# Linear attention: the low-rank gate input by 32-column products on the unnormalized state

## The chip, the cores and the metric

One NeuronCore of a Trainium2 chip runs the whole program. The metric is the device time of one execution in microseconds, the median of several runs. TensorE (PE) multiplies, VectorE (DVE) and ScalarE (ACT) do the elementwise work, GpSimd (POOL) some sums and roots, and SyncE (SP) issues most transfers.

## The reference

A trunk of two layers over 16 meta tokens and 512 tokens, width 1024. Each layer is feed-forward, mixer, feed-forward, each of them with RMSNorm before and after. The first layer's mixer is the gated linear attention that the change touches:

```python
hn = rmsnorm(h, g[2])
q, k, v, r, lr = jnp.split(hn @ w_in, ...)          # 512, 512, 1024, 1024 and 16 columns
gk = log_sigmoid(lr @ w_gate + b_gate) / 16         # 512 columns: 4 heads of 128
bcum = cumsum(gk)                                   # within chunks
q_dec, k_dec = q * exp(bcum), k * exp(-bcum)
o = causal(q_dec @ k_dec.T) @ v + q_dec @ states    # states carried from chunk to chunk
o = rmsnorm(o, g_head) * silu(r)                    # per head, 256 columns each
mix = o @ w_out
```

The 16 columns `lr` are the low-rank input of the forget gate. All four heads need the gate before anything else of theirs can begin.

## The kernel before

The state is kept transposed: tile `H` has 128 rows (a slice of the width), 8 such blocks (`KD`), and 528 tokens in columns. Tokens are worked in two groups, 272 and 256 (`L0`).

**Exactness.** The large products are made of three passes: weights and activations are each split into a rounded part and a rest (`split_part`, L233 on ScalarE, L234 on VectorE; for activations `Operand.build`), and high x high, low x high, high x low are added in PSUM. `mm3s` issues them. `mm` issues one product; a tile of plain float32 goes through it as well.

**The norm.** `Operand.build` multiplies the state by the gain of its row block only. The factor 1/rms of each token is made beside the products (`sumsq`, `factors`, `root`, `rstd`) and multiplied in when a result leaves PSUM (`x.rt`, in the traces `R_l0m`). `x.rjob` are the jobs that deliver it for each group.

**Weights.** `units` lists all weight tiles in order of use. A unit of the attention is 128 columns of `w_in`, 512 KB, fetched by two transfers on the SP queue into a ring of 8 raw tiles, split into two pair tiles, and released after use. `GLA_ORDER` gives the order: 24 is the low-rank unit (16 columns, padded to 128), 0 to 3 are the queries, 4 to 7 the keys, 8 to 15 the value tiles (two for each head), 16 to 23 the output gates `r`.

**Order of work.** TensorE's list is written out by hand. `Flow` is a virtual clock: every product adds its planned cost, and jobs (generators) resume when their `yield` is due, so their products land between those of the main line. For the other engines a scheduler sets the order. On the chip the lists are fixed, and each engine works through its own, waiting where it must.

**The attention.** `gla` begins with `x_first`: four units at once, the first group for all four, then the second group, since the state's second half arrives late. Then `x_units` takes unit after unit (both groups, 48 products each). Beside this run:

- `gates`: waits until the low-rank columns have been evacuated, multiplies them with `w_gate` (tiles `z`), and makes log-sigmoids for all heads (`ls`).
- `core(h)`, one job for each head, each waiting for the gates, its values and the head before it: cumulative sums, transposes of the values (`pv`), decays, transposes of the keys (`pk`), scores (`pa`, `pb`), chunk states (`ps`), outputs (`po`, `pn`), then the head's RMSNorm: squares (`acc_go`), their sums by twelve products with one column (`st_go`), a root in ten small steps and a diagonal (`dg_go`), and a product that spreads it over the rows (`r_go`). For the last head the root is made on VectorE, for the others on GpSimd.
- `gated(m)`: evacuates an output-gate unit (`rg`), applies tanh (L1040 to L1042), waits for the head's core, and makes the split operand `og` (L426, L427).

After the last `r` unit `out_proj` multiplies `og` with the output weights (tiles `y`). While the x units last, their products fill TensorE between the steps of the cores.

Of the kernel before, what the change touches and what calls it, by code (L numbers as in the profile page):

```python
# [13 lines left out]
ALU = mybir.AluOpType  # L14
AX = mybir.AxisListType

P = 128
D = 1024
KD = 8
# [9 lines left out]
L0 = [(0, 272), (272, 256)]  # L29
# [17 lines left out]
LONGER = 0.8  # L47
BEHIND = 2.2
NORM = 4.0
LAG = 5  # L50
PERIOD = 3.2
SLOWER = 4.0
# [5 lines left out]
V_GAIN = 0  # L58
# [2 lines left out]
V_GN = 108  # L61
V_SINK = 110
V_N = 126
GLA_ORDER = [24, 4, 0, 8, 9, 5, 1, 10, 11, 6, 2, 12, 13, 7, 3, 14, 15] + list(range(16, 24))


class Flow:
# [63 lines left out]
def trunk_kernel(ctx: ExitStack, tc, a, out):  # L131
    nc = tc.nc
    pe, act, dve, pool, sp = nc.tensor, nc.scalar, nc.vector, nc.gpsimd, nc.sync
    flow = Flow()
# [7 lines left out]
    H = cp.tile([P, KD, TOK], F32, name="H")  # L142
    Y = cp.tile([P, KD, TOK], F32, name="Y")
    vec = cp.tile([P, V_N], F32, name="vec")
# [12 lines left out]
    def duo(name):  # L157
        t = pair_tile(name, F32)
        return t[:, 0], t[:, 1]
# [355 lines left out]
    def x_units(x, nu, groups, evac):  # L515
        late = []

        def drain(i, g, p):
            for job in x.rjob:
                yield job  # L520
            evac(i, g, p)

        raw = x.column is not None

        for i in range(nu):
            w = next_w()
            pst = [ps(f"x{used[0]}_{gi}") for gi in range(len(groups))]
            for k in range(KD):
                for g, p in zip(groups, pst):
                    mm3(p[:, : g[1]], w, k, x.tiles[k], g, k == 0, k == KD - 1)  # L530
            done_w()
            for g, p in zip(groups, pst):
                if raw or all(job.done for job in x.rjob):
                    evac(i, g, p)
                else:
                    late.append(flow.spawn(drain(i, g, p)))
        return late
# [313 lines left out]
    def gla(x, finish):  # L851
        set_ahead(10)
        with tc.tile_pool(name="gp", bufs=1) as gp:
            wg, att = duo("wg")
            wg = wg[:, :512]
# [8 lines left out]
            def resets():  # L864
# [2 lines left out]
                    pool.memset(mt[:, META::st], 0.0)  # L867
                pool.memset(att, 0.0)
                yield 0
            lr = duo("lr")[0]  # L870
            qk, ls = {}, {}

            def evac(kind, h, g, p):
                o, n = g
                r = x.rt[:, o : o + n]
                if kind == "lr":
                    dve.tensor_tensor(lr[:, o : o + n], p[:, :n], r, op=ALU.mult)
                elif kind in "qk":
                    if h not in qk:
                        qk[h] = duo(f"qk{h}")  # L880
                    d = qk[h][kind == "k"][:, o : o + n]
                    if kind == "q":
                        dve.scalar_tensor_tensor(d, p[:, :n], 128 ** -0.5, r, op0=ALU.mult, op1=ALU.mult)
                    else:
                        dve.tensor_tensor(d, p[:, :n], r, op=ALU.mult)
                else:
                    dve.tensor_tensor(Y[:, h, o : o + n], p[:, :n], r, op=ALU.mult)

            def gates(drained):
                for j in drained:  # L890
                    yield j
                yield 0.8
                mns = duo("ls01") + duo("ls23")
                pairs = [pair_tile(f"az{i}", F32) for i in range(2)]
                for i, az in enumerate(pairs):
                    for h in (2 * i, 2 * i + 1):
                        b = vec[:, V_BG + h : V_BG + h + 1]
                        for o, n in L0:
                            p = ps(f"z{h}_{o}")
                            mm(p[:, :n], wg[:, h * P : (h + 1) * P], lr[:, o : o + n])  # L900
                            act.activation(az[:, h % 2, o : o + n], p[:, :n], AF.Abs, bias=b)
                            dve.tensor_scalar(mns[h][:, o : o + n], p[:, :n], b, 0.0, op0=ALU.add, op1=ALU.min)
                    last = act.activation(az, az, AF.Tanh, scale=0.5)
                    yield 1.0
                for i, az in enumerate(pairs):
                    log = act.activation(az, az, AF.Ln, scale=0.5, bias=bhalf)
                    after(last, log)
                    for h in (2 * i, 2 * i + 1):
                        dve.tensor_tensor(mns[h], mns[h], az[:, h % 2], op=ALU.add)
                        ls[h] = mns[h]  # L910
                yield 2.0
# [135 lines left out]
                dve.scalar_tensor_tensor(gs, gs, gn, Y[:, m, o : o + n], op0=ALU.mult, op1=ALU.mult)  # L1047
                split(og[m], gs, g)

            kinds = [("lr", 0), ("k", 0), ("q", 0), ("v", 0)]  # L1050
            drained = x_first(x, 4, lambda i, g, p: evac(*kinds[i], g, p), first_ahead=5)
            flow.spawn(resets())
            gate = flow.spawn(gates(drained))
            late = x_units(x, 1, L0, lambda i, g, p: evac("v", 1, g, p))
            for h in range(HEADS):
                cores.append(flow.spawn(core(h, [gate] + late + cores[h - 1 : h])))
                if h + 1 < HEADS:
                    kk = [("k", h + 1), ("q", h + 1), ("v", 2 * h + 2), ("v", 2 * h + 3)]
                    late = x_units(x, 4, L0, lambda i, g, p, kk=kk: evac(*kk[i], g, p))
# [73 lines left out]
    def swa(x, kv, finish):  # L1133
        kz, vt, dv, vmz = kv
        cap[0] = used[0] + 8
        with tc.tile_pool(name="ap", bufs=1) as ap:
# [109 lines left out]
            def core(i):  # L1246
                yield softs[i]
                yield NORM
                u, hf = visits[i]
# [71 lines left out]
    x = Operand("l0f0", lambda k: gain(0, 0, k), L0, parts=(2, 2))  # L1321
# [54 lines left out]
    x = nxt  # L1376
    nxt, fin = into("l0f1", 0, 3, False, lambda k: gain(0, 4, k), L0)
    gla(x, fin)
    x = nxt
# [4 lines left out]
    with tc.tile_pool(name="kp", bufs=1) as kp:  # L1384
        x = Operand("l1f0", lambda k: gain(1, 0, k), L1)
# [12 lines left out]
        x = nxt  # L1398
# [16 lines left out]
def _tiles(w, kt, mt):  # L1415
    return w.reshape(kt, P, mt, P).transpose(2, 1, 0, 3).reshape(mt, P, kt * P)


def _layout(x, meta_tokens, norm_gains, w_ffn_in, w_ffn_out, gla_w_in, gla_w_gate, gla_b_gate, gla_norm,
            gla_w_out, kv_norm, w_kv, swa_w_q, swa_sinks, swa_w_out):  # L1420
    c = {}
    c["h"] = np.concatenate([meta_tokens, x[0]], axis=0).T.reshape(KD, P, TOK).transpose(1, 0, 2)
    c["w_in"] = (
        w_ffn_in.reshape(2, 2, KD, P, 2, NFF, P).transpose(0, 1, 5, 4, 3, 2, 6).reshape(2, 2, NFF, 2, P, D)
    )
    wo = w_ffn_out.reshape(2, 2, NFF, P, KD, P).transpose(0, 1, 4, 3, 2, 5)
    c["w_out"] = wo[:, :, :, :, :LAST].reshape(2, 2, KD, P, LAST * P)
    c["w_last"] = (
        wo[:, :, :, :, LAST:].transpose(0, 1, 2, 4, 3, 5).reshape(2, 2, NLAST, KD, P, P)
        .transpose(0, 1, 2, 4, 3, 5).reshape(2, 2, NLAST, P, D)  # L1430
    )
    gin = np.zeros((D, 25 * P), np.float32)
    gin[:, : gla_w_in.shape[2]] = gla_w_in[0]
    c["gla_in"] = _tiles(gin, KD, 25)
    wg = np.zeros((P, 512), np.float32)
    wg[:16] = gla_w_gate[0]
    c["w_gate"] = wg
    c["gla_out"] = _tiles(gla_w_out[0], KD, KD)
    c["w_kv"] = _tiles(w_kv, KD, 4)
    c["w_q"] = (  # L1440
        swa_w_q[0].reshape(KD, P, 2, 2, 4, 64).transpose(2, 4, 1, 0, 3, 5).reshape(KD, P, D)
    )
    c["swa_out"] = (
        swa_w_out[0].reshape(2, 2, 4, 64, 4, 2, P).transpose(0, 4, 1, 3, 5, 2, 6).reshape(KD, P, D)
    )
    vec = np.zeros((P, V_N), np.float32)
    vec[:, V_GAIN : V_GAIN + 96] = norm_gains.reshape(96, P).T
    vec[:, V_KVN : V_KVN + 8] = kv_norm.reshape(8, P).T
    vec[:, V_BG : V_BG + 4] = gla_b_gate[0].reshape(4, P).T
    vec[:, V_GN : V_GN + 2] = gla_norm[0].reshape(2, P).T  # L1450
    vec[:, V_SINK : V_SINK + 16] = np.broadcast_to(
        swa_sinks[0].reshape(2, 2, 4).transpose(0, 2, 1).reshape(1, 16), (P, 16)
    )
    c["vec"] = vec
    i, j = np.arange(P)[:, None], np.arange(P)[None, :]
    c["ident"] = np.eye(P, dtype=np.float32)
    c["gmask"] = ((i <= j) & (i // 64 == j // 64)).astype(np.int32)
    c["mgt"] = (j > i).astype(np.int32)
    c["mle"] = (i <= j).astype(np.float32)
    c["rowmask"] = (i // META == np.arange(8)[None, :]).astype(np.float32)  # L1460
    ang = np.arange(TOK, dtype=np.float32)[:, None] * np.array(INV_FREQ, np.float32)[None, :]
    cos, sin = np.cos(ang).T.astype(np.float32), np.sin(ang).T.astype(np.float32)
    ct, st = np.ones((P, TOK), np.float32), np.zeros((P, TOK), np.float32)
    for r in (0, 64):
        ct[r : r + 8], ct[r + 8 : r + 16] = cos, cos
        st[r : r + 8], st[r + 8 : r + 16] = -sin, sin
    c["cos"], c["sin"] = ct, st
    c["sel"] = np.zeros((P, 32), np.float32)
    for e in range(2):
        c["sel"][64 * e : 64 * e + 16, 16 * e : 16 * e + 16] = np.eye(16)  # L1470
    c["cosp"], c["sinp"] = np.tile(np.concatenate([cos, cos]), (8, 1)), np.tile(np.concatenate([-sin, sin]), (8, 1))
    return {n: np.ascontiguousarray(v) for n, v in c.items()}
# [20 lines left out]
```

## Time and profile before

| | us |
|---|---|
| median of 3 runs | 1905.15 (1903.95 to 1905.66) |
| profiled execution | 1903.94 |
| its span in the trace | 1902.2 |
| TensorE busy | 1878.5 |
| VectorE busy | 1403.7 |
| ScalarE busy | 1016.8 |
| attention: first x product to first output product | 375.8 to 577.4 |

Busy times are unions over the span; a row of the timeline gives start, length, engine, line, operation, result and operands, and the number of records. A product of plain float32 leaves two records, one of the split kind leaves one. A pair such as 128*32 after MATMUL is rows and columns of the array in use. A few records can be missing.

### The profile page before, as it was taken

What the parts mean: (1) busy time and instruction counts of PE and PEld (TensorE: products, weight loads), DVE (VectorE), ACT (ScalarE), POOL (GpSimd) and SP (SyncE); (2) the same over time, 40 slices, a digit from 0 to 9 for tenths busy, and PEclk for the clock granted to TensorE, in tenths of its full rate; (3) what the DMA queues carried; (4) which work ended last, traced back from release to release, by engine and by line L of the source; (5) the groups of instructions that cost most, each with busy time, mean ns of one, the idle gap of its engine ahead of it and who ended that gap; (6) DMA issues with size and microseconds to landing.
All of it is one profiled execution on the core that took longest, in us unless ns stands there. A gap on an engine that the chain in (4) does not pass through costs nothing.

```text
span 1902.2 us, 37641 instructions
## 1 busy us (share of the span) xinstructions
PE 1878.5 (99%) x14642; PEld 1796.4 (94%) x14642; DVE 1403.7 (74%) x2825; ACT 1016.8 (53%) x2268; POOL 187.8 (10%) x374
## 2 busy tenths in 40 slices
PE   8999999999999999999999999999999999999997
PEld 8999999999999999999999898989987798989897
DVE  7885858766574798585887886868766779868584
ACT  5663635653245566363674553535756755636363
POOL 2000000321111300000033000000320140000002
PEclk9999999999999999999999999999999999999999
DMA  4333333422123123333351223233421212333331
GB/s 166 98 97 98 97 105 98 126 79 73 50 63 105 46 88 92 94 103 98 101 172 45 67 89 112 92 110 99 134 73 51 68 45 73 105 104 107 101 112 45
DMA packets 102931, 175.13 MB, mean 92 GB/s; under 512 B 11872, under 2 KB 24928, under 8 KB 102752
## 3 DMA queue, kind: packets, MB, share of 16 engines
q1 hardware_dynamic: 101920, 172.07, 28.8%
q8 instruction: 115, 1.88, 0.4%
q10 hardware_dynamic: 832, 0.65, 0.1%
q14 instruction: 64, 0.52, 0.1%
HBM read 170.05 MB, written 2.10 MB: 91 GB/s over the span
## 4 chain that ended last, share of the span: by engine, by line
PE 86%; DVE 10%; ACT 2%; issue 2%; DMA 0%; POOL 0%; DVEq 0%; ACTq 0%; POOLq 0%
PE y L169 29%; PE x L169 18%; PE a L169 18%; PE c L169 8%; PE d L169 4%; DVE raw L258 2%; PE o L169 1%; ACT w_s L252 1%; DVE w_s L253 1%; DVE w L253 1%; PE e L169 1%; DVE w L234 1%; PE po L169 1%; PE sa L169 1%; PE ps L169 0%
## 5 line engine op out<-in xcount | busy, mean ns | idle before, releaser
L253 DVE TENSOR_TENSOR w_s<-raw,w_s 128x512 fp32r<-128x512 f32 x288 | 193.9, 691 | 130.5 <-ACT w_s L252 128.1
L169 PE MATMUL y<-hidl0f,w 128*128 128x256 f32 (+1 forms) x2112 | 262.3, 285 | 1.1 <-DVE hidl0f L427 0.8
L169 PEld LDWEIGHTS y<-hidl0f,w 128*128 128x128 f32 x2112 | 259.2, 188 | 2.2 <-DVE hidl0f L427 1.5
L252 ACT ACTIVATE w_s<-raw 128x512 fp32r<-128x512 f32 x288 | 175.1, 628 | 151.5 <-DVE raw L258 138.5
L234 DVE TENSOR_TENSOR w<-raw,w 128x512 fp32r<-128x512 f32 x378 | 236.4, 656 | 21.8 <-ACT w L233 19.9
L169 PE MATMUL y<-hidl1f,w 128*128 128x512 f32 (+1 forms) x1344 | 250.9, 346 | 0.4 <-DVE hidl1f L844 0.2
L169 PEld LDWEIGHTS y<-hidl1f,w 128*128 128x128 f32 x1344 | 212.5, 188 | 35.0 <-DVE hidl1f L844 1.6
L233 ACT ACTIVATE w<-raw 128x512 fp32r<-128x512 f32 x378 | 207.5, 586 | 40.1 <-PE y L169 29.3
L422 POOL TENSOR_TENSOR acc_post<-acc_post,sq_post 128x256 f32<-128x256 f32 (+1 forms) x77 | 63.2, 821 | 1473.1 <-ACT sq_post L421 1472.4
L258 DVE TENSOR_TENSOR raw<-raw,raw 128x512 f32<-128x512 f32 x288 | 198.0, 688 | 5.5
L253 DVE TENSOR_TENSOR w<-raw,w 128x512 fp32r<-128x512 f32 x216 | 148.4, 688 | 29.9 <-ACT w L252 29.1
L169 PE MATMUL x<-x_l0m,w 128*128 128x272 f32 (+1 forms) x1200 | 158.2, 288 | 0.0
L252 ACT ACTIVATE w<-raw 128x512 fp32r<-128x512 f32 x216 | 134.0, 621 | 41.3 <-PE y L169 41.0
L169 PEld LDWEIGHTS x<-x_l0m,w 128*128 128x128 f32 x1200 | 149.3, 189 | 1.0
L621 DVE TENSOR_TENSOR Y<-y,Y 128x256 f32<-128x256 f32 (+2 forms) x176 | 82.4, 474 | 73.1 <-PE y L169 72.6
L169 PE MATMUL a<-zl0f_t,w_s 128*128 128x264 f32 x864 | 117.3, 285 | 0.0
L169 PE MATMUL a<-zl1f_t,w_s 128*128 128x256 f32 x864 | 114.7, 282 | 0.8 <-ACT c L819 0.6
L169 PEld LDWEIGHTS a<-zl0f_t,w_s 128*128 128x128 f32 x864 | 110.2, 188 | 0.2
L169 PEld LDWEIGHTS a<-zl1f_t,w_s 128*128 128x128 f32 x864 | 107.4, 188 | 2.7 <-ACT c L819 2.2
L169 PE MATMUL x<-x_l0f,w 128*128 128x256 f32 (+1 forms) x768 | 100.3, 291 | 6.4 <-ACT w L233 5.8
L169 PEld LDWEIGHTS x<-x_l0f,w 128*128 128x128 f32 x768 | 97.1, 193 | 7.5 <-ACT w L233 5.8
L169 PE MATMUL x<-x_l1f,w 128*128 128x256 f32 (+1 forms) x576 | 93.1, 321 | 0.0
(497 smaller groups left out, 3249.0 us busy)
## 6 DMA issues: line engine op xcount, KB each, us to landing
raw<-in_w_in SPq DMA_DIRECT2D x352, 256.0 KB, 2.9
raw<-in_w_out SPq DMA_DIRECT2D x96, 256.0 KB, 3.4
raw<-in_gla_in SPq DMA_DIRECT2D x50, 256.0 KB, 3.2
raw<-in_w_last SPq DMA_DIRECT2D x48, 256.0 KB, 3.1
raw<-in_w_out SPq DMA_DIRECT2D x64, 128.0 KB, 2.9
raw<-in_gla_out SPq DMA_DIRECT2D x16, 256.0 KB, 2.8
raw<-in_w_q SPq DMA_DIRECT2D x16, 256.0 KB, 4.1
raw<-in_swa_out SPq DMA_DIRECT2D x16, 256.0 KB, 3.2
```

The source lines that it names most:

```text
L169: inst = pe.matmul(o, lhs, rhs, start=start, stop=stop, skip_group_check=onto)
L233: act.activation(w[:, 0, :m], raw[:, :m], AF.Copy)
L234: dve.tensor_tensor(w[:, 1, :m], raw[:, :m], w[:, 0, :m].bitcast(F32), op=ALU.subtract)
L252: act.activation(w[:, 0, :512], src, AF.Copy)
L253: dve.tensor_tensor(w[:, 1, :512], src, w[:, 0, :512].bitcast(F32), op=ALU.subtract)
L258: dve.tensor_tensor(dst, dst, src, op=ALU.add)
L422: pool.tensor_tensor(sums[0][:, :n], sums[0][:, :n], t[:, :n], op=ALU.add)
L621: dve.tensor_tensor(y, p[:, :n], y, op=ALU.add)
```

## The change

The low-rank columns are no longer a unit. Their weights come as 1024 x 32 columns (16 of them zeros) in a transfer of their own into the free half of tile `lr`; VectorE multiplies the gains into them. Then 16 plain float32 products, 8 row blocks for each token group, read the state `H` itself. Row blocks 0 to 3 go to four column strips of the array and four row strips of a PSUM bank, blocks 4 to 7 are added to them. The four partial sums are not added there: `w_gate` is laid out four times, 32 rows each, so that the gate product adds them. The evacuation multiplies by 1/rms, after waiting for both groups' factors.

In `x_first` the freed place is taken by the first head's second value tile, which had a pass of `x_units` of its own, so 24 units remain instead of 25. The gates wait for the new job as well.

```diff
-GLA_ORDER = [24, 4, 0, 8, 9, 5, 1, 10, 11, 6, 2, 12, 13, 7, 3, 14, 15] + list(range(16, 24))
+GLA_ORDER = [4, 0, 8, 9, 5, 1, 10, 11, 6, 2, 12, 13, 7, 3, 14, 15] + list(range(16, 24))
...
-            lr = duo("lr")[0]
+            lr, low = duo("lr")
+            low = low[:, : KD * 32].rearrange("p (k c) -> p k c", c=32)
+            sp.dma_start(low, a["w_low"])
...
-                if kind == "lr":
-                    dve.tensor_tensor(lr[:, o : o + n], p[:, :n], r, op=ALU.mult)
-                elif kind in "qk":
+                if kind in "qk":
...
+            def low_rank():
+                gains = vec[:, V_GAIN + 16 : V_GAIN + 16 + KD]
+                dve.tensor_tensor(low, low, gains.unsqueeze(2).to_broadcast([P, KD, 32]), op=ALU.mult)
+                yield LOW
+                banks = [ps(f"lr_{o}") for o, _ in L0]
+                for (o, n), p in zip(L0, banks):
+                    for k in range(KD):
+                        c = slice(k % 4 * 32, k % 4 * 32 + 32)
+                        mm(p[c, :n], low[:, k], H[:, k, o : o + n], k < 4, k >= 4, cost=0.14)
+                for job in x.rjob:
+                    yield job
+                for (o, n), p in zip(L0, banks):
+                    dve.tensor_tensor(lr[:, o : o + n], p[:, :n], x.rt[:, o : o + n], op=ALU.mult)
...
-            kinds = [("lr", 0), ("k", 0), ("q", 0), ("v", 0)]
+            kinds = [("k", 0), ("q", 0), ("v", 0), ("v", 1)]
             drained = x_first(x, 4, lambda i, g, p: evac(*kinds[i], g, p), first_ahead=5)
             flow.spawn(resets())
-            gate = flow.spawn(gates(drained))
-            late = x_units(x, 1, L0, lambda i, g, p: evac("v", 1, g, p))
+            gate = flow.spawn(gates(drained + [flow.spawn(low_rank())]))
+            late = []
...
-    gin = np.zeros((D, 25 * P), np.float32)
-    gin[:, : gla_w_in.shape[2]] = gla_w_in[0]
-    c["gla_in"] = _tiles(gin, KD, 25)
-    wg = np.zeros((P, 512), np.float32)
-    wg[:16] = gla_w_gate[0]
-    c["w_gate"] = wg
+    c["gla_in"] = _tiles(gla_w_in[0][:, : 24 * P], KD, 24)
+    low = np.zeros((D, 32), np.float32)
+    low[:, :16] = gla_w_in[0][:, 24 * P :]
+    c["w_low"] = low.reshape(KD, P, 32).transpose(1, 0, 2)
+    wg = np.zeros((4, 32, 512), np.float32)
+    wg[:, :16] = gla_w_gate[0]
+    c["w_gate"] = wg.reshape(P, 512)
```

More of the change, by code (lines that the diff above doesn't have):

```diff
@@ L49 @@
 NORM = 4.0
+LOW = 1.0
 LAG = 5
```

## The prediction

> **What bounds the kernel now.** I read the page first: the shares of busy time, then the chain that ended last.
>
> ```profile
> PE 1878.5 (99%) x14642; PEld 1796.4 (94%) x14642; DVE 1403.7 (74%) x2825; ACT 1016.8 (53%) x2268; POOL 187.8 (10%) x374
> PE 86%; DVE 10%; ACT 2%; issue 2%; DMA 0%; POOL 0%; DVEq 0%; ACTq 0%; POOLq 0%
> ```
>
> TensorE works for 99% of the span and is 86% of the chain. The waits of TensorE inside the attention stage (376 to 592 us) have one entry:
>
> ```profile
> PE y L169 <- DVE og L427: 0.4, 1, 0.4
> ```
>
> So in this stage a product that goes is time won, as long as something else stands where it stood; a product that covered a chain on another engine is not.
>
> **The unit that goes.** The low-rank columns were one of 25 units of 128 columns; a unit is 48 products (3 passes, 8 row blocks, two token groups). The timeline of TensorE has an undisturbed stretch of such products:
>
> ```profile
> 403.33 6.83 PE L169 MATMUL x<-x_l0m,w 128*128 128x272 f32 x54
> 410.00 0.59 PE L169 MATMUL r_l0m<-dg_l0m,ones 128*128 128x256 f32 x2
> ```
>
> 54 products fill 403.33 to 410.00, 0.123 us each; 48 of them are **-5.9 us**. The first head's second value unit only changes its place (from alone to within x_first), with the same 48 products. Two fewer splits on VectorE and ScalarE and 0.5 MB less on the queue are off the path.
>
> **The 16 products that come.** They are plain float32, 128 rows by 32 columns, four of them in four column strips. The trace has this shape once, in the rotary turn, and the unpacked float32 shape in the gates:
>
> ```profile
> 1392.89 0.64 PE L169 MATMUL turn<-q,sel 128*32 128x256 f32 x8
> 1393.46 1.80 PE L169 MATMUL x<-x_l1m,w 128*128 128x256 f32 x13
> 1441.75 1.07 PE L169 MATMUL turn<-q,sel 128*32 128x512 f32 x8
> 417.70 1.94 PE L169 MATMUL z<-lr,wg 128*128 128x272 f32 x8
> 419.30 4.36 PE L169 MATMUL x<-x_l0m,w 128*128 128x256 f32 x33
> ```
>
> Eight records are four products (two records each). Packed, four take 0.57 us from their start to the next work (1393.46 - 1392.89); unpacked, four take 1.60 (419.30 - 417.70). So the strips do run side by side, and four groups of four cost 4 x 0.57 = **+2.3 us**. The lower end is 4 x 0.43 = 1.7 us, 0.43 being what 256 more columns cost the group (1.07 - 0.64); the upper end is 4 x 1.60 = 6.4 us. I take 2.3, the row of the same shape. The gate products keep number and size: the four partial sums are added by the repeated gate weights.
>
> **What they wait for.** The weights come by a transfer queued on SP behind that of the gate weights, into a slot freed some two microseconds later; VectorE then multiplies in the gains.
>
> ```profile
> 360.83 0.33 SPq L856 DMA_DIRECT2D wg<-in_w_gate  x1
> 394.30 27.97 SPq L301 DMA_DIRECT2D raw<-in_gla_in  x14
> DMA to landing us min/median/max: 2.7/2.7/2.7
> 378.71 0.50 DVE L448 SCALAR_TENSOR_TENSOR x_l0m<-H,vec,x_l0m 128x272 fp32r<-128x272 f32 x1 [0.65 <-ACT x_l0m L447]
> 380.89 0.16 DVE L372 TENSOR_SCALAR av_post_l0m<-st_post_l0m 128x2 f32<-128x2 f32 x1 [1.68 <-PE st_post_l0m L169]
> ```
>
> The built list puts the multiplication between the two VectorE rows, into 1.68 us of idle time, some 12 us after the landing; 128x256 costs about 0.47, by size from the 0.50 of 128x272. Queued behind it is the whole second residual chain, so a late landing would be dear, but it would have to be 12 us late. On SP the next transfer does not start before 394.30. Both cost nothing. The evacuation of the first partial sums stands on VectorE ahead of the next key evacuation, which has to wait for TensorE anyway; two units' splits now lie behind that wait, but three units of 5.9 us stand ahead of their use. The two PSUM banks that the partial sums hold until the second scale arrives are given to the next unit but one, which comes later. Nothing again.
>
> **What the unit was covering.** Here the change costs. The four heads run one after another, each a chain of steps that become due on a planned clock; the x products are laid between them. The gates still start the first head, but one unit fewer stands beside the heads, so the x products run out earlier while the heads do not. This is the end of the last head before, on TensorE:
>
> ```profile
> 568.72 3.55 PE L169 MATMUL x<-x_l0m,w 128*128 128x272 f32 x27
> 572.12 1.98 PE L169 MATMUL st_go<-ones,acc_go 128*68 128x1 f32 x24
> 573.96 2.79 PE L169 MATMUL x<-x_l0m,w 128*128 128x256 f32 x21
> 576.62 1.16 PE L169 MATMUL r_go<-dg_go,ones 68*128 68x272 f32 x4
> 577.43 2.12 PE L169 MATMUL y<-og,w 128*128 128x272 f32 x14
> 579.91 20.34 PE L169 MATMUL y<-og,w 128*128 128x272 f32 x162 [0.35 <-DVE og L427]
> ```
>
> and on VectorE:
>
> ```profile
> 573.24 0.16 DVE L372 TENSOR_SCALAR av_go<-st_go 68x4 f32<-68x4 f32 x1 [4.10 <-PE st_go L169]
> 574.21 0.16 DVE L372 TENSOR_SCALAR av_go<-st_go 128x2 f32<-128x2 f32 x1 [0.81 <-PE st_go L169]
> 574.29 0.36 DVE L375 TENSOR_SCALAR yv_go<-av_go 68x4 int32<-68x4 int32 x2
> 576.14 0.76 DVE L401 TENSOR_TENSOR dg_go<-hident,yv_go 68x272 f32<-68x272 f32 x2
> 578.13 0.77 DVE L1042 SCALAR_TENSOR_TENSOR rg<-rg 128x272 f32<-128x272 f32 x2
> 579.42 1.45 DVE L427 TENSOR_TENSOR og<-rg,og 128x272 fp32r<-128x272 f32 x4
> 583.45 1.28 DVE L234 TENSOR_TENSOR w<-raw,w 128x512 fp32r<-128x512 f32 x2
> ```
>
> st_go sums the squares, VectorE turns them into a root in ten small dependent steps and a diagonal (dg_go), and r_go spreads it. Before, 21 x products lie between st_go and r_go and cover this to within 0.1 us. In the changed program's list for TensorE nothing lies there: the last x product stands ahead of st_go, r_go right behind it. Worse, VectorE's list has put other work between the ten steps: two gating products (L1042), two splits of 128x512 and four subtractions for og, which before stood outside.
>
> Count from the start of st_go. Its 24 records last 1.84 us (572.12 to 573.96), the second sum reaches VectorE at 2.09, r_go starts at 4.50 (576.62). The inserted work adds 2 x 0.35 (0.77 less the overlap of one) + 2 x 0.60 (1.28 - 0.68) + 4 x 0.35 (1.45 / 4) = 3.3 us, less 0.3 because six steps no longer wait for the step before them (two steps in about 0.15 instead of 0.2; 574.29 to 576.14 is nine times 0.2). So r_go starts at 7.5 and TensorE is idle for 7.5 - 1.84 = 5.66, **+5.6 us**. Bounds: 2.7 if nothing were inserted, 6.2 if nothing is saved and a split is late. In exchange og of two value tiles is ready early, and the wait of 0.35 at 579.91 with its restart goes: **-0.5 us**. What is late next is og of the last head; 54 output products stand ahead of it, 6.6 us, as before, when VectorE had more to do on that path and TensorE's waits still had no entry for it but the one above. No wait.
>
> **The clock.** An idle TensorE does one more thing here. Windows of 3.41 us laid on the edges at which the granted clock changes:
>
> ```profile
> core 0: us, PE busy (x), PEclk, DMA share, GB/s
> 572.29:575.71 3.42, 3.42 (x37) 1.00 0.00 0
> 1517.79:1521.20 3.41, 2.53 (x30) 1.00 0.00 0
> 1521.20:1524.61 3.41, 3.41 (x17) 0.50 0.00 0
> 1524.61:1528.02 3.41, 3.41 (x30) 1.00 0.00 0
> 1889.84:1893.25 3.41, 0.85 (x7) 1.00 0.00 0
> 1893.25:1896.67 3.42, 1.08 (x2) 0.50 0.00 0
> ```
>
> After a window with 0.9 us of idle time and many small products the next one ran at 0.50: 17 records instead of 30, so 43% of 3.41 us, about 1.5, was lost. After one that was mostly idle it was 0.50 too. 5.6 us of idle time hold at least one mostly idle window, wherever the edges fall. The slow time ends at the first edge after a busy window, which leaves 1.2 to 4.9 us of work at half speed, 0.5 to 2.1 us lost: **+1.5 us**. The Trainium skill, TensorE: Matmul & The Clock Gate, What's actually happening, says that the array falls to half rate after an idle window of about 3.4 us and that the window runs free of the kernel; the rows above agree, and it speaks against this change. By its figure alone, half of one window of 3.4 us, the term would be 1.7, an estimate, and the sum +3.2.
>
> **The sum**: -5.9 + 2.3 + 5.6 - 0.5 + 1.5 = +3.0 us. The profiled execution took 1903.94 us (span 1902.2), 1.2 under the median of 1905.15; on the median the forecast is **1908.1 us**, +0.16%. A measurement of this kernel can tell about 0.2% from no change, 3.8 us, so 1901.3 to 1909.0 counts as the same.
>
> **The rivals.**
> 1. The clock holds: everything else as above, 1906.6. For it: the window at 572.29 with st_go in it did not lower the clock. Against it: 5.6 us without any product. Chance 0.20.
> 2. Slower: the edges fall so that the half clock lasts two windows, or the inserted work runs to its upper end. Place: the first output products after r_go. It decides from 0.8 us above my sum: 6.2 of idle time instead of 5.6 with 2.1 lost to the clock gives +4.2, 1909.3; 1909.9 if the early og wins nothing, and 1910.5 with 0.6 of new waits at other steps of the heads, whose places among the x products move too. Chance 0.32.
> 3. The strips do not overlap with eight different weights: +6.4 instead of +2.3, 1912.2. The turn loads the same selector four times, here each strip has its own weights; the loads are separate in both. Chance 0.08.
> 4. The change does just what it says: r_go finds its diagonal ready. -5.9 + 2.3 - 0.5 = -4.1, 1901.0, faster by 0.2%. The order of the two lists speaks against it. Chance 0.06.
>
> **How the numbers follow.** The forecast itself has 0.34. Faster is rival 4: 0.06. The same is the forecast and rival 1: 0.54. Slower is rivals 2 and 3: 0.40. The range leaves out rivals 3 and 4 (0.14): its low end is rival 1 less 0.6 for the idle time, 0.5 for the products and 1.2 for the spread of runs, 1904.3; its high end rival 2's 1910.5 and 0.5 of spread, 1911.0.
>
> **What would show it.** Right: 24 x units; 32 records of 128*32 in about 2.2 us after st_l0m near 403; in the waits of TensorE r_go on VectorE's dg_go with 5 to 6 us, the largest of the stage; the og wait gone; the granted clock at 0.50 for one or two windows near 580 to 588. Wrong: no such wait, or x products between st_go and r_go; strips that start 0.4 us apart; a wait of the low products on their weights; waits elsewhere in the stage of over 1 us.

## The result and the profile after

The changed kernel takes **1908.3 us** (median of 22 runs, 1906.3 to 1909.2); the kernel before took 1904.26 in the runs beside it (22 runs, 1902.5 to 1905.7). The ratio is 1.0019, 95% interval 1.0013 to 1.0025: slower by an amount just at what can be told. The profiled execution took 1908.11 us (1903.94 before), its span is 1906.0.

Executions of one kernel differ by a few us, and those with the lower mean granted clock of TensorE are the longer ones, so each run below is read by its profile as well.

Busy times and the chain of the changed kernel:

```profile
PE 1875.4 (98%) x14626; PEld 1791.9 (94%) x14626; DVE 1400.4 (73%) x2824; ACT 1015.2 (53%) x2266; POOL 189.2 (10%) x374
PE 85%; DVE 9%; ACT 3%; issue 2%; POOL 1%; DMA 0%; SPq 0%; DVEq 0%; ACTq 0%; POOLq 0%
```

TensorE has 16 records fewer (48 of the unit are gone, 32 of the low-rank products have come) and is busy 3.1 us less, in an execution that is 4.2 us longer. So it waits more. Its waits in the attention stage are these two:

```profile
PE r_go L170 <- DVE dg_go L402: 5.4, 1, 5.4
PE r_go L170 <- POOL dg_go L402: 1.4, 1, 1.4
```

The first is the forecast stall, the largest of the stage; the wait of y on og is gone. The second, of the third head's r_go, was not foreseen. The timeline of TensorE at the low-rank products, the third head and the last head:

```profile
403.47 1.99 PE L170 MATMUL lr<-H,lr 128*32 128x272 f32 x32
405.39 4.30 PE L170 MATMUL x<-x_l0m,w 128*128 128x272 f32 x33
...
544.06 2.00 PE L170 MATMUL r_go<-dg_go,ones 68*128 68x272 f32 x4 [1.43 <-POOL dg_go L402]
545.85 1.06 PE L182 MATMUL pv<-ident,Y 128*128 128x128 f32 x4
...
574.66 1.98 PE L170 MATMUL st_go<-ones,acc_go 128*68 128x1 f32 x24
582.01 2.13 PE L170 MATMUL r_go<-dg_go,ones 68*128 68x272 f32 x4 [5.37 <-DVE dg_go L402]
583.57 8.71 PE L170 MATMUL y<-og,w 128*128 128x272 f32 x59
```

The 16 products take 1.92 us (405.39 - 403.47). No x product lies between st_go and r_go; r_go starts 7.35 us after st_go. The two r_go take 2.13 us against 1.16 before: TensorE is at half speed. Windows laid on the edges of the granted clock show it:

```profile
core 0: us, PE busy (x), PEclk, DMA share, GB/s
541.60:545.01 3.41, 1.85 (x12) 1.00 0.42 147
545.01:548.42 3.41, 3.41 (x14) 0.50 0.00 0
548.42:551.84 3.42, 3.42 (x31) 1.00 0.00 0
575.73:579.14 3.41, 0.91 (x9) 1.00 0.00 0
579.14:582.56 3.42, 0.55 (x1) 0.50 0.48 153
582.56:585.97 3.41, 3.41 (x13) 0.50 0.00 0
585.97:589.38 3.41, 3.41 (x30) 1.00 0.10 11
```

After the last head's stall there are two windows at half speed; the work from 582.01 to 585.97 took 4.0 us and would have taken 2.0. One more follows the third head's wait, with 14 records where the next has 31. The window at 1521 that the kernel before lost in its profile is absent here.

### The profile page after: what moved, and what is told of

Its sections match the earlier page's. It is cut to its first block, busy times and chain, and to the rows that moved or that the text cites. A ratio compares the mean times of both kernels' runs of the same rounds, so it can differ in the third digit from the quotient of the medians.

```text
span 1906.0 us, 37601 instructions
## 1 busy us (share of the span) xinstructions
PE 1875.4 (98%) x14626; PEld 1791.9 (94%) x14626; DVE 1400.4 (73%) x2824; ACT 1015.2 (53%) x2266; POOL 189.2 (10%) x374
## 4 chain that ended last, share of the span: by engine, by line
PE 85%; DVE 9%; ACT 3%; issue 2%; POOL 1%; DMA 0%; SPq 0%; DVEq 0%; ACTq 0%; POOLq 0%
PE y L170 31%; PE x L170 18%; PE a L170 17%; PE c L170 7%; PE d L170 4%; DVE raw L259 2%; ACT w_s L253 2%; PE o L170 1%; DVE w_s L254 1%; DVE w L254 1%; PE e L170 1%; DVE w L235 1%; PE po L170 1%; PE sa L170 1%; DVE hidl1f L845 1%
## 5 line engine op out<-in xcount | busy, mean ns | idle before, releaser
L170 PE MATMUL x<-x_l0m,w 128*128 128x272 f32 (+1 forms) x1152 | 152.8, 289 | 0.0
L170 PEld LDWEIGHTS x<-x_l0m,w 128*128 128x128 f32 x1152 | 144.2, 190 | 1.4 <-issue 0.4
```

What stands on the lines that cost most here:

```text
L170: inst = pe.matmul(o, lhs, rhs, start=start, stop=stop, skip_group_check=onto)
```

## The experiments

The medians below stand beside a kernel before of 1903.8 to 1904.3; each ratio is to the kernel before, with its 95% interval.

**Busy instead of idle.** Useless products in the stall:

```diff
         yy = root(sq, n, dim, name, eng)
+        if fill:
+            p = ps(f"fill_{name}")
+            for i in range(fill[0]):
+                mm(p[:, :256], fill[1][:, 0, :P], fill[2][:, 0, :256], cost=1e-9)
```

> The changed kernel, with 44 useless products of the split kind (128x256, 0.117 us each, 5.15 us together) put on TensorE between the last head's sums st_go and its spreading products r_go; their bank is read by nobody. If the idle time costs its own length and, through the granted clock, two more windows at half speed: the wait of r_go falls from 5.4 to about 0.2 us, the clock stays at 1.00 near 579 to 586, and the time falls by what those windows lose, r_go 0.3 and the output products 1.6 us, to about 1906.4. If the idle time costs only its length: the same time as the changed kernel, 1908.3, with busy time in place of the wait. If the filler delays r_go (it is not what r_go waits for): over 1909.

Measured: 1907.57 us (1905.2 to 1908.6), ratio 1.0019 (1.001 to 1.0028); profiled 1906.69. TensorE in its profile:

```profile
574.92 5.51 PE L170 MATMUL fill_go<-x_l0m,x_l0m 128*128 128x256 f32 x44
580.53 1.13 PE L170 MATMUL r_go<-dg_go,ones 68*128 68x272 f32 x4
```

r_go runs at full speed, it no longer waits, and no window of the stage is at half. The time from st_go to r_go is about the same (7.45 us for 7.35), and the profiled execution is 1.4 us shorter than that of the changed kernel: there three windows of the stage are at half and none near 1521, here none of the stage and one at 1523. One of the three isn't the filler's doing: the third head's wait of 1.4 us is still there, and this time no slow window follows it. In the medians the gain is 0.7 us: five of the eleven runs had the mean clock 0.995 and took 1908 to 1908.6. So the profile shows that the idle time brought the slow windows at the last head; what they cost in the medians lies between the two expectations and is not settled by this run.

**The order on VectorE.**

```diff
+                inst = dve.scalar_tensor_tensor(gs, th, 1.0, gs, op0=ALU.add, op1=ALU.mult)
+                if m == 7:
+                    behind_root(inst)
...
+        if i in (83, 84):
+            behind_root(inst)
...
+                if m in (4, 5):
+                    behind_root(inst)
```

`behind_root` orders an instruction behind the last head's second diagonal. The first place is the gating products, the second the splits of two weight units, the third the subtractions that split og.

> The changed kernel, with the eight pieces of VectorE work that stand between the steps of the last head's root (two gating products, two weight splits, four subtractions of og) ordered behind its diagonal; nothing is left out. If they make up half of the stall: the wait of r_go falls from 5.4 to 2.5 to 2.7 us, one half-clock window instead of two, and the time falls by 2.7 to 4.5 us, to 1903.8 to 1905.6, unless og of two value tiles comes late, which would show as a wait of the output products of 0.5 to 1.5 us. If the root's steps are the whole of it and the inserted work fills only their gaps: the wait stays above 5 us and the time at 1908.3.

Measured: 1905.21 us, ratio 1.0010 (1.0001 to 1.0019). TensorE's waits in the stage and three windows:

```profile
PE r_go L170 <- DVE dg_go L412: 2.5, 1, 2.5
PE r_go L170 <- POOL dg_go L412: 1.4, 1, 1.4
...
573.07:576.48 3.41, 3.11 (x35) 1.00 0.00 0
576.48:579.89 3.41, 1.20 (x3) 0.50 0.00 0
579.89:583.31 3.42, 3.42 (x15) 0.50 0.48 134
```

The stall is 2.5 for 5.4: the eight pieces of other work are 2.9 us of it, and the ten steps themselves the rest. TensorE's waits show no late og. The median fell by 3.1 us against the changed kernel, within the 2.7 to 4.5 expected; two windows at half remain at the last head, one more than expected, while the one at the third head is absent from this profile, so the 3.1 are not the stall alone.

**The strips.**

```diff
-                        c = slice(k % 4 * 32, k % 4 * 32 + 32)
-                        mm(p[c, :n], low[:, k], H[:, k, o : o + n], k < 4, k >= 4, cost=0.14)
+                        c = slice(0, 32)
+                        mm(p[c, :n], low[:, k], H[:, k, o : o + n], k == 0, k == KD - 1, cost=0.14)
```

> The changed kernel with all 16 low-rank products in one column strip: eight row blocks are added in rows 0 to 31 of the bank, and evacuation and gate products use these 32 rows alone. If the strips run side by side in the changed kernel (1.92 us for 16): 16 x 0.40 = 6.4 us, 4.5 us more, 1912.8, since everything behind them is later by as much. If the strips give nothing: 1908.3 and a group of 1.9 us as before.

Measured: 1912.98 us (5 runs), ratio 1.0051 (1.0039 to 1.0064), 4.7 over the changed kernel. The low-rank products and what follows them on TensorE:

```profile
403.58 7.31 PE L170 MATMUL lr<-H,lr 128*32 128x272 f32 x32
410.81 4.30 PE L170 MATMUL x<-x_l0m,w 128*128 128x272 f32 x33
```

In one strip they take 7.23 us, 0.45 each, where four strips take 1.92. The strips do run side by side with different weights: rival 3 falls.

**The first part of the change alone.**

```diff
-            kinds = [("k", 0), ("q", 0), ("v", 0), ("v", 1)]
-            drained = x_first(x, 4, lambda i, g, p: evac(*kinds[i], g, p), first_ahead=5)
+            kinds = [("k", 0), ("q", 0), ("v", 0)]
+            drained = x_first(x, 3, lambda i, g, p: evac(*kinds[i], g, p), first_ahead=5)
...
-            late = []
+            late = x_units(x, 1, L0, lambda i, g, p: evac("v", 1, g, p))
```

> Only the first part of the change: the low-rank products as in the changed kernel, but the first head's second value tile back in a pass of its own beside the gates, so that three units run at the state's late arrival instead of four. If what the change loses is the cover of the last head: 21 x products stand again between st_go and r_go, no wait of over 0.5 us there and none at the third head, no half clock in the stage, -5.9 + 1.9 against the kernel before, 1900.3; to that comes what TensorE waits for the state's second half in the shorter first pass (it gets there near 388, and VectorE hands out its eight blocks from 387.4 to 395 or 399): 1 to 5 us, so 1901.3 to 1905.3. If the loss lies in the low-rank products themselves (late gates, clock): 1908 or more with the stall where it is.

Measured: 1902.51 us (1901.5 to 1906.1), ratio 0.9998 (0.9989 to 1.0007); profiled 1901.53. Its waits in the stage, the last head, and two windows:

```profile
PE x L170 <- ACT x_l0m L448: 2.2, 2, 2.0
PE y L170 <- DVE og L428: 0.4, 1, 0.4
...
574.62 2.79 PE L170 MATMUL x<-x_l0m,w 128*128 128x256 f32 x21
577.27 1.16 PE L170 MATMUL r_go<-dg_go,ones 68*128 68x272 f32 x4
...
392.73:396.14 3.41, 1.52 (x11) 1.00 0.42 142
396.14:399.55 3.41, 3.06 (x14) 0.50 0.38 114
```

With the 21 x products back both r_go waits are gone. The loss lies in the place of the value unit, not in the low-rank products. But the shorter first pass meets the state's second half too early, with 2.2 us of waiting and a half-clock window. In these two orders the value unit covers one hole or the other: the late state or the last head's root.

**The third head.** Only the last head's two cumulative sums are put behind the third head's scaling:

```diff
+                if last:
+                    after(spread[-1], s64)
+                    after(spread[-1], s128)
```

> The changed kernel with the last head's two cumulative sums on VectorE (1.25 and 1.23 us, at 541.2 to 543.6) ordered behind the third head's scaling by r_go; nothing else. If they slow GpSimd's root beside them (its step 1.13 and its diagonal 1.63 us under them, against 0.19 and 0.64 in the kernel before): these go back to under 0.7, the third head's r_go waits under 0.3 us instead of 1.4, no half clock near 545, and with the last stall as it is the time falls by 0 to 2 us, since the last head's chain comes later by what it waits for its sums. If GpSimd's steps are slow for another reason: the wait stays above 1 us.

Measured: 1908.25 us, ratio 1.0019 (1.001 to 1.0028). Two steps of GpSimd's root and the sums on VectorE in the changed kernel, below the dots the same two steps in this run, and last the end of that root and the sums in the kernel before:

```profile
541.18 1.25 DVE L940 TENSOR_TENSOR_SCAN b<-resets,ls 128x528 f32<-128x528 f32 x1
541.28 1.13 POOL L392 TENSOR_SCALAR zv_go<-zv_go 128x2 f32<-128x2 f32 x1
542.35 1.23 DVE L941 TENSOR_TENSOR_SCAN b<-resets,ls 128x528 f32<-128x528 f32 x1
542.38 1.63 POOL L402 TENSOR_TENSOR dg_go<-hident,yv_go 68x272 f32<-68x272 f32 x1
...
541.53 0.18 POOL L392 TENSOR_SCALAR zv_go<-zv_go 128x2 f32<-128x2 f32 x1
541.68 0.63 POOL L402 TENSOR_TENSOR dg_go<-hident,yv_go 68x272 f32<-68x272 f32 x1
...
542.04 0.68 POOL L401 TENSOR_TENSOR dg_go<-hident,yv_go 128x256 f32<-128x256 f32 x1
543.33 1.25 DVE L922 TENSOR_TENSOR_SCAN b<-resets,ls 128x528 f32<-128x528 f32 x1
545.17 1.25 DVE L923 TENSOR_TENSOR_SCAN b<-resets,ls 128x528 f32<-128x528 f32 x1
```

Each of the two slow steps of GpSimd starts within 0.1 us of a sum and ends with it or 0.4 later; without the sums the steps are 0.18 and 0.63, and the wait is gone. So the cause of the second wait is shown; before, the sums came when the root was done. The Trainium skill, SBUF — State Buffer, Who interferes with whom, says that a VectorE instruction with two inputs in SBUF contends with a GpSimd instruction that reads SBUF, through a shared read port that is locked exclusively; the rows agree.

The median did not fall. In this profile r_go of the last head starts at 578.71 instead of 582.01, 3.3 us earlier, behind the same stall of 5.37. But the windows there are

```profile
571.00:574.41 3.41, 2.34 (x29) 1.00 0.00 0
574.41:577.82 3.41, 0.00 (x0) 0.50 0.39 145
577.82:581.24 3.42, 2.53 (x7) 0.50 0.02 8
581.24:584.65 3.41, 3.41 (x17) 0.50 0.00 0
```

and two more at half stand at 1523.3 to 1530.1, in a profiled execution of 1908.74 us. Two of eleven runs took 1904.4 and 1905.2, the others 1907.5 to 1909.6 at a lower mean clock. In the profile what was won was lost to the clock: 1.0 more behind the stall (4.4 us of work at half from 580.27 on, 2.4 from 583.57 in the changed kernel), and up to 3.4 at 1523, where the changed kernel's profile has none. Why most runs lose it is open.

**Useful work in the stall.** Four banks of the output product are begun with the first two heads' og behind the last head's sums, then continued with the third head's. It is tried on the changed kernel, on the changed kernel with both orders of the experiments above, and on the kernel before; on the changed kernel the planned time of r_go moves as well, to where its diagonal is ready:

```diff
-            flow.wait(*jobs[:12])
+            flow.wait(*jobs[:8])
...
+            if early:
+                flow.wait(*jobs[:12])
+                set_ahead(16)
+                cap[0] = used[0] + 12
+                for m, g in order[:ahead_of]:
+                    go_on(m, g, range(early, nh - late))
...
-                    eng, more = (dve, gi * BEHIND) if last else (pool, BEHIND)
+                    eng, more = (dve, 2.0 + gi) if last else (pool, BEHIND)
```

> The changed kernel with useful work in the stall: after the last head's st_go TensorE begins four banks of the output product with the value tiles og of the first two heads (48 products, 5.6 us, most of them ahead of r_go), then adds those of the third head, and waits for the last head only then; nothing is left out. If the change's loss is the missing cover: the wait of 5.4 us falls under 1, no half clock near 579 to 586, and against the changed kernel (1907.6 to 1908.3) 5.4 and 2 us go, 1901 to 1902, less up to 1.5 if og of the last head is now waited for; the third head's wait of 1.4 us on GpSimd stays. If the stall only moves, because the last head's og is as late as before and the output products in front of it are used up: a wait of 3 us of y on og, 1904 to 1905.

> The same cover, and also the eight pieces of VectorE work ordered behind the last head's diagonal and the last head's two scans ordered behind the third head's scaling by r_go. If cover, order and the scans are what TensorE lost: no wait of over 0.5 us in the stage, no half clock in it, -5.9 + 1.9 - 0.4 against the kernel before (1903.8 to 1904.3), 1899.4 to 1899.9, and 1900.5 at most. If the waits only move: 1901.5 or more, with a new wait on og or on the last head's cumulative sums.

> The cover alone on the kernel before, which has 21 x products at the place: it has only the wait of 0.35 us of y on og to win. If the cover's worth in the changed kernel comes from the stall that the change makes: 1903.3 to 1904.3, the same as before within 0.5 us. If starting the output products early is worth something by itself: under 1902.5.

Measured: 1906.91, 1902.01 and 1904.36 us; ratios 1.0009 (1.0 to 1.0019), 0.999 (0.9982 to 0.9999) and 1.0 (0.9991 to 1.0009). The first missed what was expected by 5 us although the stall was gone, the second by 1.5; the third came out without a change, as expected. The waits of the stage behind the attention, in the first of the three, and below the dots two rows of VectorE in the second:

```profile
PE r_post_l0f L170 <- DVE dg_post_l0f L402: 2.2, 1, 2.2
PE y L170 <- DVE hidl0f L428: 0.3, 1, 0.3
...
621.20 1.29 DVE L235 TENSOR_TENSOR w<-raw,w 128x512 fp32r<-128x512 f32 x2
625.47 1.28 DVE L235 TENSOR_TENSOR w<-raw,w 128x512 fp32r<-128x512 f32 x2
```

All three have the wait of r_post_l0f (2.2 to 2.3 us), with one or two half-clock windows from 635 on. The edit had counted the weight units allowed ahead (`cap`) after two had been taken, so four splits (the two rows) came to stand in the residual chain of the next stage. Neither expectation had named this. The next runs count from before, `cap[0] = used[0] + 10`:

> The cover alone (as in the first cover run), but the weight units allowed ahead during the output products are counted from before the four banks are begun, so that no splits fall into the residual chain of the next stage (four stood there at 621 to 627, and its r_post_l0f waited 2.2 us). If the first cover run lost its gain there: this wait goes, with one or two windows of half clock behind it, 2.2 to 4 us, 1902.9 to 1904.7; the third head's 1.4 us stay. If the gain was lost elsewhere: 1906 to 1907 again.

> Cover, order of the root and of the scans, with the same count of weight units. If nothing else is hidden: no wait of over 0.4 us in the stage and the next, no half clock before 1500, and the sum of the change alone, -5.9 + 1.9 - 0.4, against the kernel before: 1899.5 to 1900.5, faster than both kernels. If half clock has other causes than these waits: 1902 as without the new count.

> The same cover and count on the kernel before. If all they do is to fill a stall that this kernel doesn't have: 1903.3 to 1904.4, no change. If they are worth something without the change: under 1902.5.

Measured: **1901.06** us (ratio 0.9987, 0.9978 to 0.9996), **1900.01** (0.998, 0.9972 to 0.9989; 1898.7 to 1900.5) and 1902.67 (0.9992, 0.9983 to 1.0001). The wait of r_post_l0f is gone in all. The first came out 1.8 us under the lower end of what was expected, although the third head's wait stays; its profile has no window at half before 1889. The waits of the second of these, from 370 to 700 us, and its last head:

```profile
PE y L170 <- DVE hidl0f L442: 0.3, 1, 0.3
PE y L170 <- ACT og L441: 0.2, 1, 0.2
...
571.72 1.98 PE L170 MATMUL st_go<-ones,acc_go 128*68 128x1 f32 x24
573.57 3.16 PE L170 MATMUL y<-og,w 128*128 128x272 f32 x24
576.56 0.62 PE L170 MATMUL r_go<-dg_go,ones 68*128 68x272 f32 x2
```

This version came out as expected and beats both kernels, 0.2% under the one before and 8.3 us under the change as it was made, and its executions lie closest together. Its profile has no window at half before 1887. Its profiled execution takes 1898.80, 5.1 less than that of before; -5.9 + 1.9 - 0.4 and another 1.5 for the window at 1521 would be 5.9 less. On the kernel before, cover and count were expected to change nothing; whether the 1.1 us in the medians are more than that stays open, since the interval holds 1. Against the kernel before with the same cover and count, the second version is 2.7 us shorter, and its longest execution (1900.5) is under the other's shortest (1900.8).

## Why the prediction was right, and where it was not

- **The unit, -5.9**: 24 units are left; the version without waits shows it only together with the next term, 3.8 us under before in the medians where -4.4 were due with og. Up to 1.1 of the 3.8 may belong to the cover, as the run of the cover on the kernel before leaves open.
- **The 16 products, +2.3**: 1.92. The strips overlap; the upper end of 6.4 would have been 7.2.
- **Their waits, nothing**: TensorE has no wait on the weights or the evacuations.
- **The stall, +5.6**: 5.37. Its parts are shown apart: inserted work 2.9 (worked as 3.0), the chain alone 2.5 (worked as 2.7).
- **og, -0.5**: the wait is gone.
- **The clock, +1.5**: two windows in the profile, 2.0 us, near the upper end of 0.5 to 2.1, and part of what rival 2 described. Rival 1, that the clock holds, falls. Three readings behind the term were too simple. The slow time does not always end after a busy window: in the third-head run 1523.30 to 1526.72 was at half and busy throughout, and the next window was at half too. Nor are 4.9 us of slow work an upper bound: that run has 5.9 behind its stall (578.71 to 584.65). And the prediction finds its rows in agreement with a fall after an idle window, but the window ahead of 1521.20 was busy for 2.53 of its 3.41 us and so was not an idle one.
- **Missed**: the third head. The prediction named waits of over 1 us elsewhere as a sign against it, and one is there, with a window at half. The step that failed is the comparison of VectorE's order, made at the last head's root alone and not beside the roots on GpSimd; new waits at other heads stood in rival 2 with 0.6, in the forecast with nothing. The rows have 1.4 of wait, and up to 1.7 of a half-clock window; st_go of the last head starts 1.6 us later than in the run with the filler (574.66 against 573.08), which has the wait without the window.
- **The sum**: -5.9 + 1.9 + 5.4 - 0.5 + 2.0 for the clock, + 1.4 + 1.7 at the third head, - 1.5 for the window at 1521: +4.5; the profiled executions differ by 4.2, the medians by 4.0. Forecast were +3.0 from 1905.15. That 1908.1 lies so near 1908.3 is luck in part: the forecast missed 1.0 us of the change, and its starting median, of three runs, was 0.9 above the later 1904.26.
- **Rival 4** (r_go finds its diagonal ready) describes what the cover makes of the change: -4.1 was its price, 1901.0 from the starting median; measured were 1901.06 and 1900.01, which is -2.7 and -3.8 from the kernel before beside them. As an account of the change as it was made it falls, with the stall.

## What to carry to other kernels

Work that is removed ahead of a chain of dependent steps is won only if the chain moves ahead as well, or if other work takes the place: count the products that stand beside each step in both lists, and look for work of the next stage that is ready. Compare the order on every engine at every step of the chain, not at the last one alone. When work is begun earlier, look at everything that is counted from its beginning, here the weights allowed ahead.

## What the runs showed of the hardware

The clock falls after less idle time than a whole window. It was at 0.50 in the window after one with 1.85 of 3.41 us busy (changed kernel), after 2.34 (the third-head run), and after 3.11 (the run with the order on VectorE), where 24 of the 35 records were the sums' products with one column. Yet it stayed at 1.00 after a window with 1.99 (542.34 to 545.76 in the run with the order on VectorE) and one with 2.16 (540.80 to 544.21 in the cover with the early count). So the profile's busy time alone does not decide; what is counted no run here shows. The Trainium skill, TensorE: Matmul & The Clock Gate, What's actually happening, speaks of an idle window; the windows before the clock fell were not idle by the profile's busy time, and the measurement decides.

The same 1.43 us of wait at the third head cost a window in the changed kernel's profile and none in that of the cover with the early count. That the place of the edges decides this is likely, but not shown: in the run with the order on VectorE the whole wait lies in one window, and the clock held. Executions of one kernel differ by as much as the change moves: the changed kernel from 1906.3 to 1909.2 us, the third-head run from 1904.4 to 1909.6.

In one column strip, products added one after another, eight for each group, took 0.45 us each (7.23 us for 16), more than the 0.40 of unpacked products of full width in the gates.
